# Splitting the second score products of two attention maps over the two halves of TensorE's rows

## The chip, the cores and the metric

The kernel runs on one core of a Trainium2 chip. The metric is the device time in microseconds (us) of one execution, from the median of several runs. The core has five engines that run side by side, each in the order of its own instructions: TensorE does matrix products (PE in the profile, its weight loads are PEld), VectorE does elementwise work and reductions (DVE), ScalarE does activations and copies (ACT), GpSimd does small elementwise work and indirect transfers (POOL), and SyncE issues most transfers (SP). They wait for each other through semaphores.

## The reference, cut to what matters

The reference is a two-layer transformer on 256 image tokens and 256 context tokens of width 1024. Each layer normalizes and modulates the tokens, projects them, runs three kinds of attention heads in parallel, projects back, and runs a mixture of 16 experts. The change lies in the scores of the attention:

```
def diff_attention(q, k, v, lam):          # "A" heads: two maps each
    s = jnp.einsum('bhiqd,bhikd->bhiqk', qb.astype(jnp.float32), kf) * scale
    p = jax.nn.softmax(s, axis=-1)
    w = p[:, :, 0] - lam * p[:, :, 1]
...
def gqa_attention(q, k, v, sink=None):     # "B" heads: two query heads share a key head
    s = jnp.einsum('bhgqd,bhkd->bhgqk', qb.astype(jnp.float32), kf) * scale
...
def window_attention(q, k, v, kc, vc, sink):   # "C" heads: a band mask, and a sink
```

All of it is in float32, with heads of 64 dimensions. Layer 0 computes attention for the context tokens too; layer 1 only for the image tokens.

## The kernel before, in words

The tokens lie in four tiles of 128: tiles 0 and 1 are the context, tiles 2 and 3 the image. A context tile attends to 256 keys (`nk` = 2 blocks), an image tile to 512 (`nk` = 4). Attention is cut into items: one `AItem` per query tile and A head (two maps), one `BItem` per query tile and pair of B or C heads (two maps as well). Layer 0 has 32 items, of which the second 16 are of image tiles; layer 1 has 16, all of image tiles. So 32 items have 512 keys.

Products of float32 are made from parts. A number is split into a high part, rounded to the kernel's float32r, and a low part, the rest. For the keys, `to_T` (L874) writes for map `i` the high part of the 64 dimensions into one half of the 128 partitions (the half `64*i`) and the low part into the other half. For the queries, both halves of the partitions hold the same 64 dimensions; `Item.high` (L1446) makes their high part and `Item.low` (L1453) their low part, both on GpSimd. One product over 128 rows with the high part of the queries thus gives high times high plus high times low; a second one with the low part of the queries gives low times high plus low times low. `Item.maps` (L1457) does this: for each of the two maps it makes the two products one after the other into the map's PSUM bank (L1466), and for masked C items it then adds the mask with a small bf16 product over 128 columns (L1470). The context items put both maps into one bank; the image items take two banks.

The scores' banks come from a ring of three (`PS_ATT`, L47, `sc=3`), and an image item takes two, so that one of its two maps has to wait until the exponentials of an earlier map have left its bank.

After the scores, `maxima` (L1472) reduces each map over its keys on VectorE (L1480, one instruction per map for 512 keys), then scales the maxima (L1486, or L1483 and L1484 with a sink). `exps` (L1488) runs the exponentials on ScalarE (L1493). `weights` combines the maps (L1534 for A items) or normalizes them (L1619, L1620), `transposes` turns them on TensorE (`tp`, L193), `evacuate` copies them out, and `values` multiplies them with the values (`poA`, L1549, in tiles of 128x128 of the array; `poB`, L1640, in tiles of 128 rows by 64 columns).

The order is written out by hand in `attention` (L954) with `TICK` (L65). In each tick TensorE gets, in this order: the transposes of item n, the transposes of an earlier tile's end (`onA`) where there are any, the scores of item n + 3, the values of item n - 1, and then some units of other work, the modulation products `ada` (L459, 128 rows by 32 columns of the array), as many as `fill` deals out. So right after an image item's scores TensorE meets `poA` or a transpose (the whole array), or `poB` or `ada` (the array cut by columns). VectorE gets in each tick the sums and weights of item n first, and then the maxima of item n + 3.

One product elsewhere has the form that the change brings: near the end of layer 1, `add` (L1274) adds the ninth group of experts with `sT[s]` and `y[s]` (L1282), where `s` is the lower or the upper 64 rows in turn, each into a bank of its own.

Of the kernel before, what the change touches and what calls it, by code (L numbers as in the profile page):

```python
# [1429 lines left out]
class Idle:  # L1430

    high = low = weights = scores = transposes = maxima = evacuate = exps = sums = values = staticmethod(lambda: None)
# [3 lines left out]
class Item:  # L1436
# [20 lines left out]
    def maps(self, kT, k, mask=None):  # L1457
        m, nc = self.m, self.nc
        if self.nk == 2:
            self.banks = [m.bank("sc").rearrange("p (i n) -> p i n", i=2)]  # L1460
            self.ps = [self.banks[0][:, i] for i in range(2)]
        else:
            self.ps = [m.bank("sc"), m.bank("sc")]
        for i, ps in enumerate(self.ps):
            for n, part in enumerate(self.hl):
                nc.tensor.matmul(ps, lhsT=part[:, i], rhs=kT[:, k, i, :self.nkey],  # L1466
                                 start=n == 0, stop=n == 1 and mask is None)
            if mask is not None:
                c, v = mask
                nc.tensor.matmul(ps[:, c * 128:c * 128 + 128], lhsT=m.k["identb"], rhs=v, start=False, stop=True)  # L1470

    def maxima(self):  # L1472
# [538 lines left out]
```

## Time and profile before

| | |
|---|---|
| median of 3 runs | 889.74 us (887.74 to 889.86) |
| the profiled execution | 888.22 us |
| its span, from the first to the last instruction | 886.3 us |
| TensorE busy | 784.3 us, 88% of the span |
| VectorE busy | 582.4 us, 66% |
| ScalarE busy | 447.6 us, 50% |
| GpSimd busy | 222.2 us, 25% |
| granted TensorE clock, mean | 0.95 of full speed |

Busy time says how long an engine had something in it; since products overlap in the array, a busy TensorE is not one at its peak. What sets the time is read from the chain of work that ended last, which goes back from the last instruction to whatever released it, step by step. Start times are counted from the beginning of the span. A timeline row of several instructions gives the first start and the time to the last end, so that the distance between the starts of two rows, not their lengths, tells how long the first kept the engine from the second.

### The profile page before, as it was taken

The numbers are of one execution on the slowest core, as the hardware profiler recorded it, in microseconds if no ns is written. First come the engines' busy times: TensorE is split into PE (matmuls) and PEld (weight loads), VectorE is DVE, ScalarE is ACT, GpSimd is POOL, SyncE is SP. The second block draws the span as 40 slices with busy tenths as digits, with TensorE's granted clock in tenths as the row PEclk, the third lists the DMA queues.
The fourth block names the chain that finished last, engine by engine and source line by source line (L and its number), as shares of the span: only waits on it lengthen the run. The fifth ranks groups of instructions, "written<-read, shape, count | busy, mean of one in ns | idle before, by whom it ended". The sixth has DMA issues, their size and how long they took to land.

```text
span 886.3 us, 12972 instructions
## 1 busy us (share of the span) xinstructions
PE 784.3 (88%) x4731; PEld 576.3 (65%) x4731; DVE 582.4 (66%) x1200; ACT 447.6 (50%) x861; POOL 222.2 (25%) x258
## 2 busy tenths in 40 slices
PE   4899999889989977999999549998899797999984
PEld 0578878445557746999999438887555565656541
DVE  1577673879863798899999586697667566221226
ACT  2454442667773416888888546462466543111112
POOL 2000101556320133443342472100423101000200
PEclk9999999999999988999999859999899997999987
DMA  9952221667879337899993757342188955999981
GB/s 319 344 185 96 95 96 48 247 270 284 275 214 376 121 148 263 306 388 401 400 408 156 249 195 292 128 158 95 51 331 215 340 186 215 350 423 422 419 333 51
DMA packets 54505, 219.18 MB, mean 247 GB/s; under 512 B 10299, under 2 KB 10299, under 8 KB 36640
## 3 DMA queue, kind: packets, MB, share of 16 engines
q1 hardware_dynamic: 40816, 182.34, 55.0%
q0 software_dynamic: 8736, 24.92, 7.9%
q10 hardware_dynamic: 4880, 11.00, 3.2%
q8 instruction: 39, 0.64, 0.3%
q14 instruction: 34, 0.28, 0.1%
HBM read 207.09 MB, written 16.84 MB: 253 GB/s over the span
## 4 chain that ended last, share of the span: by engine, by line
PE 66%; DVE 16%; DMA 8%; ACT 3%; issue 3%; POOL 2%; SPq 0%; ACTq 0%; POOLq 0%; DVEq 0%
PE mm L207 7%; PE mm L206 7%; PE mm L205 7%; PE tp L193 6%; PE gu L1189 6%; PE ada L459 4%; PE gu L207 4%; PE gu L205 3%; PE gu L206 3%; DMA wraw<-in_w_up 3%; PE sc L1466 3%; PE w L1245 3%; DVE wlo L235 2%; PE w L1154 2%; DVE nm L1480 2%
## 5 line engine op out<-in xcount | busy, mean ns | idle before, releaser
L235 DVE TENSOR_TENSOR wlo<-wraw,whi 128x1024 fp32r<-128x1024 f32 x136 | 186.1, 1392 | 43.0 <-ACT whi L234 40.5
L234 ACT CAST whi<-wraw 128x1024 fp32r<-128x1024 f32 x152 | 152.8, 1050 | 57.7 <-PE mm L207 35.5
L205 PE MATMUL mm<-whi,Xh 128*128 128x512 f32 x288 | 116.3, 405 | 5.1 <-ACT Xh L690 4.7
L206 PE MATMUL mm<-wlo,Xh 128*128 128x512 f32 x288 | 115.3, 400 | 0.5 <-DVE wlo L235 0.5
L207 PE MATMUL mm<-whi,Xl 128*128 128x512 f32 x288 | 115.0, 399 | 0.5 <-DVE Xl L694 0.5
L221 POOL TENSOR_TENSOR rstd<-ms,cst 128x1 f32<-128x1 f32 (+2 forms) x34 | 29.4, 864 | 272.1 <-DVE ms L219 263.2
L1493 ACT ACTIVATE e<-sc,nm 128x512 f32<-128x512 f32 (+1 forms) x96 | 58.4, 613 | 42.4 <-DVE nm L1486 22.6
L207 PE MATMUL gu<-whi,xl 128*128 128x256 f32 x256 | 74.3, 290 | 0.0
L205 PE MATMUL gu<-whi,xh 128*128 128x256 f32 x256 | 74.2, 290 | 0.0
L206 PE MATMUL gu<-wlo,xh 128*128 128x256 f32 x256 | 72.7, 284 | 0.0
L1189 PE MATMUL gu<-wraw,xq 128*64 128x256 f32 x512 | 64.4, 396 | 3.7 <-DMA wraw<-in_w_up 3.7
L205 PEld LDWEIGHTS mm<-whi,Xh 128*128 128x128 f32 x288 | 55.1, 191 | 18.7 <-ACT Xh L690 6.2
L207 PEld LDWEIGHTS mm<-whi,Xl 128*128 128x128 f32 x288 | 55.0, 191 | 13.9 <-DVE Xl L694 1.5
L206 PEld LDWEIGHTS mm<-wlo,Xh 128*128 128x128 f32 x288 | 55.1, 191 | 12.8 <-DVE wlo L235 1.2
L235 POOL TENSOR_TENSOR wlo<-wraw,whi 128x1024 fp32r<-128x1024 f32 x16 | 42.7, 2672 | 81.1 <-ACT whi L234 50.3
L1189 PEld LDWEIGHTS gu<-wraw,xq 128*64 128x64 f32 x512 | 37.9, 142 | 24.1 <-DMA wraw<-in_w_up 4.2
L193 PEld LDWEIGHTS tp<-ident,e 128*128 128x128 f32 x240 | 26.1, 142 | 40.8 <-issue 21.1
L1480 DVE TENSOR_REDUCE nm<-sc 128x1 f32<-128x512 f32 x64 | 41.2, 684 | 16.5 <-PE sc L1466 11.6
L207 PEld LDWEIGHTS gu<-whi,xl 128*128 128x128 f32 x256 | 49.3, 193 | 1.1 <-DVE xl L1050 0.4
L205 PEld LDWEIGHTS gu<-whi,xh 128*128 128x128 f32 x256 | 49.6, 194 | 0.3 <-ACT xh L1049 0.3
L206 PEld LDWEIGHTS gu<-wlo,xh 128*128 128x128 f32 x256 | 49.5, 193 | 0.0
L193 PE MATMUL tp<-ident,e 128*128 128x128 f32 x240 | 37.8, 286 | 8.4 <-DVE e L1534 3.9
(348 smaller groups left out, 1625.4 us busy)
## 6 DMA issues: line engine op xcount, KB each, us to landing
wraw<-in_w_ada SPq DMA_DIRECT2D x40, 1024.0 KB, 4.9
wraw<-in_w_gate SPq DMA_DIRECT2D x32, 1024.0 KB, 10.1
wraw<-in_w_up SPq DMA_DIRECT2D x32, 1024.0 KB, 11.0
wraw<-in_w_down SPq DMA_DIRECT2D x32, 1024.0 KB, 14.1
wraw<-in_w_in SPq DMA_DIRECT2D x14, 1024.0 KB, 5.2
wraw<-in_w_ada SPq DMA_DIRECT2D x16, 512.0 KB, 8.1
yrows<-y ACTq DMA_DIRECT2D x16, 512.0 KB, 8.1
wraw<-in_w_in POOLq DMA_DIRECT2D x5, 1024.0 KB, 11.9
```

The lines of the kernel that those rows point to most:

```text
L193: self.nc.tensor.transpose(out, in_, self.k["ident"][:n, :n])
L205: mm(out, lhsT=xh, rhs=wh, start=start, stop=False)
L206: mm(out, lhsT=xh, rhs=wl, start=False, stop=False)
L207: mm(out, lhsT=xl, rhs=wh, start=False, stop=stop)
L221: nc.gpsimd.tensor_tensor(r, ms, self.k["mhalf"][:, :width], OP.pow)
L234: nc.scalar.copy(h, raw[:, lo:hi])
L235: (engine or nc.vector).tensor_tensor(l, raw[:, lo:hi], h.bitcast(F32), OP.subtract)
L459: nc.tensor.matmul(ps[32 * j:32 * j + 32, :], lhsT=self.silu_c[:, kc, :], rhs=raw[:, 512 * j:512 * j + 512], start=kc == 0, stop=kc == NKC ...
L1189: nc.tensor.matmul(gu[PSLOTS * g:PSLOTS * g + PSLOTS, 256 * b:256 * b + 256], lhsT=xq[q][:, kc, c:c + PSLOTS], rhs=raw[:, kc * 256:kc * 25 ...
L1245: nc.tensor.matmul(y[hf][gs], lhsT=hT[:, c, 0:PSLOTS] if p == NP else hT[:, c, gs], rhs=raw[:, c * D + o * 512:c * D + o * 512 + 512], sta ...
L1480: V.reduce_max(self.nm[:, i:i + 1], self.ps[i], axis=AX.X)
L1493: nc.scalar.activation(self.e[i][:, :self.nkey], self.ps[i], AF.Exp, scale=0.125, bias=self.nm[:, i:i + 1], accum_out=self.z[i])
```

## The change

For items with 512 keys the two first products, each over 128 rows, come first, one for each map; then the two second products come, each over 64 rows: map 0 on rows 0 to 63 and map 1 on rows 64 to 127, where the high part of its keys lies. The low times low part is no longer computed there. The masks follow after both. Items with 256 keys keep their products and their order. The numbers of products, weight loads and columns stay the same.

```diff
-        for i, ps in enumerate(self.ps):
-            for n, part in enumerate(self.hl):
-                nc.tensor.matmul(ps, lhsT=part[:, i], rhs=kT[:, k, i, :self.nkey],
-                                 start=n == 0, stop=n == 1 and mask is None)
-            if mask is not None:
-                c, v = mask
+        high, low = self.hl
+
+        def product(i, part, rows, **flags):
+            nc.tensor.matmul(self.ps[i], lhsT=part[rows, i], rhs=kT[rows, k, i, :self.nkey], **flags)
+
+        if self.nk == 2:
+
+            for i in range(2):
+                product(i, high, slice(0, 128), start=True, stop=False)
+                product(i, low, slice(0, 128), start=False, stop=True)
+            return
+        for i in range(2):
+            product(i, high, slice(0, 128), start=True, stop=False)
+
+        for i in range(2):
+            product(i, low, slice(64 * i, 64 * i + 64), start=False, stop=mask is None)
+        if mask is not None:
+            c, v = mask
+            for ps in self.ps:
                 nc.tensor.matmul(ps[:, c * 128:c * 128 + 128], lhsT=m.k["identb"], rhs=v, start=False, stop=True)
```

## Rows read from the trace of the kernel before

**Rows 1.** The page's chain that ended last: shares of the span by engine.

```profile
PE 66%; DVE 16%; DMA 8%; ACT 3%; issue 3%; POOL 2%; SPq 0%; ACTq 0%; POOLq 0%; DVEq 0%
```

**Rows 2.** Busy time by stretch, image items: window, length, engines, granted clock, DMA.

```profile
197.00:264.00 67.00, 61.35 (x433) 37.67 (x433) 52.99 (x137) 49.78 (x122) 25.31 (x42) 1.00 0.76 263
626.00:689.00 63.00, 57.93 (x387) 33.63 (x385) 46.25 (x109) 39.77 (x100) 24.43 (x42) 0.95 0.67 217
...
626.00:638.00 12.00, 8.92 (x30) 4.07 (x29) 10.47 (x21) 5.06 (x14) 9.36 (x17) 0.72 0.01 1
```

**Rows 3.** The instructions of line L1466: count, shortest, median and longest ns.

```profile
L1466 PE MATMUL sc<-kT,qhl x96: 277/395/792, 154.6 to 666.4; 128*128 128x512 f32 x64, 128*128 128x256 f32 x32
...
L1466 PE MATMUL sc<-k2T,qhl x96: 277/396/792, 155.6 to 684.9; 128*128 128x512 f32 x64, 128*128 128x256 f32 x32
```

**Rows 4.** Timeline of PE around two unmasked items: start, length, line, array tile, count.

```profile
215.25 1.17 PE L1466 MATMUL sc<-kT,qhl 128*128 128x512 f32 x4
216.26 1.05 PE L1549 MATMUL poA<-vA,ptA 128*128 128x128 f32 x8
...
218.65 1.16 PE L1466 MATMUL sc<-k2T,qhl 128*128 128x512 f32 x4
219.75 1.06 PE L459 MATMUL ada<-wraw,silu_c 128*32 128x512 f32 x8
```

**Rows 5.** Timeline of PE around L1282, whole-array products and then products of 64 rows.

```profile
870.96 1.08 PE L1282 MATMUL acc<-yl,sT 128*128 128x512 f32 x4
...
871.97 0.50 PE L1282 MATMUL acc<-yh,sT 64*128 64x512 f32 x2
...
872.30 0.40 PE L1282 MATMUL acc<-yh,sT 64*128 64x512 f32 x2
```

**Rows 6.** The chain by time, dense products before layer 1's attention: start, us, what.

```profile
624.01 0.23 PE mm L205
```

**Rows 7.** Timeline of PE around a masked item.

```profile
670.34 0.71 PE L1466 MATMUL sc<-k2T,qhl 128*128 128x512 f32 x2
670.89 0.23 PE L1470 MATMUL sc<-mask,identb 128*128 128x128 bf16 x1
670.93 0.71 PE L1466 MATMUL sc<-k2T,qhl 128*128 128x512 f32 x2
671.49 0.23 PE L1470 MATMUL sc<-mask,identb 128*128 128x128 bf16 x1
671.55 0.33 PE L1549 MATMUL poA<-vA,ptA 128*128 128x128 f32 x1
```

**Rows 8.** Timeline of PE and DVE at layer 0's first image item.

```profile
197.02 1.18 PE L1466 MATMUL sc<-kT,qhl 128*128 128x512 f32 x4
...
197.77 1.29 DVE L1480 TENSOR_REDUCE nm<-sc 128x1 f32<-128x512 f32 x2 [1.39 <-PE sc L1466]
```

**Rows 9.** The chain by time, layer 0, image items.

```profile
197.77 1.30 DVE nm L1480 x2
...
204.72 1.21 DVE nm L1480 x2
...
207.03 0.73 PE sc L1466 x2
...
215.49 0.93 PE sc L1466 x4
...
218.89 0.92 PE sc L1466 x4
...
249.66 1.30 DVE nm L1480 x2
```

**Rows 10.** The chain by time, layer 1, its first image items.

```profile
629.45 0.75 PE sc L1466 x2
...
630.22 0.70 DVE nm L1480
...
632.73 1.24 DVE nm L1480 x2
...
635.21 1.22 PE sc L1466 x2
```

**Rows 11.** Timeline of PE in the same stretch, third item.

```profile
632.01 1.22 PE L1466 MATMUL sc<-k2T,qhl 128*128 128x512 f32 x2 [1.04 <-ACT e L1493]
```

**Rows 12.** Waits, layer 1's image items: who for whom, us, times, longest.

```profile
DVE nm L1480 <- PE sc L1466: 6.0, 5, 2.0
```

## The prediction

> **What bounds the kernel now.** I read the chain that ended last first: 66% of it is TensorE and 16% VectorE [rows 1]. So a product that gets cheaper can count, but only in the stretches where the change is. These are the image items of the two layers, 67 and 63 us long, with TensorE busy 61.35 and 57.93 us and VectorE 52.99 and 46.25 us [rows 2]: TensorE is nearly full, VectorE is close behind, and the chain passes between them. The line of the scores has 64 + 64 products of 512 columns [rows 3], four for each of 32 items. Half of them, 64, become products of 64 rows, that is 32 pairs; the others stay.
>
> What one item keeps TensorE from doing next is the distance between starts in the timeline. With four score products followed by `poA`, which uses the whole array, it is 216.26 - 215.25 = 1.01 us; followed by `ada`, which cuts the array by columns, 219.75 - 218.65 = 1.10 us [rows 4]. A whole-array product in a dense run takes 0.23 us [rows 6], so the first of the four takes 1.01 - 3 x 0.23 = 0.32 us, and a passage to another cut of the array costs 1.10 - 1.01 = 0.09 us. That 0.09 is the number to watch, because the new pair is another cut.
>
> **The change part by part.** The pair itself. The kernel already has such pairs, at L1282: four whole-array products from 870.96, then two products of 64 rows that both start at 871.97, then two more at 872.30 [rows 5]. Two things are to be seen. The two halves run side by side, since two take 0.50 us from start to end and the next two start 0.33 us later. And the passage costs the same 0.09: 871.97 - 870.96 - 4 x 0.23. The 0.33 instead of 0.23 is a weight load that nothing hides just after the passage. So the pair saves one product (0.23) and pays 0.09 to go in, 0.10 for the bare weight load, and 0.09 to come out, unless the next product cuts the array anyway. No row shows the way out of a pair; I take the 0.09 of the other passages, with 0 and 0.18 as ends. Beside that, the first whole-array product after the pair shows its own weight load: between 0 and the 0.10 of the pair, I take 0.05.
>
> The sum for an item on TensorE is then 0.32 (first product of map 0) + 0.23 + 0.09 (first product of map 1, passage) + 0.33 + 0.09 (pair, passage) = 1.06 us. Before `ada` or `poB` that replaces 1.10: a gain of 0.04. Before `poA` or a transpose it is 1.06 + 0.05 = 1.11 and replaces 1.01: a loss of 0.10. A masked item takes 671.55 - 670.34 = 1.21 us now [rows 7]; after, 1.06 and two masks in a row, of which the second ends 0.06 before `poA` starts as now, and the first takes 0.05 to 0.12 by the same rows: 1.17 to 1.24, which I count as 0.
>
> On the price of a passage the Trainium skill has a rule ("TensorEngine Tiling (Array Packing)", Key Properties): changing the tiling mode, not just the tile, drains TensorE. The 0.09 of rows 4 and 5 agrees that there is a price. The Trainium skill's page "TensorE: Matmul & The Clock Gate" (Step-by-step) puts the drain at about 128 cycles, an estimated 0.05 us at 2.4 GHz; with that the sum below would come out about 1 us lower. The rows measure it here, so I stay with 0.09.
>
> The order. Before, map 0 was complete after two products, and VectorE could reduce it while TensorE made map 1; now both maps are complete together, after the pair. In the first image item the reduction starts 197.77 - 197.02 = 0.75 us after the scores [rows 8]. After, it is 0.32 + 0.23 + 0.09 + 0.50 (the first pair's length) + the 0.03 that a reduction starts after the end of the product, = 1.17: 0.42 us later. Map 1 is not earlier by anything that counts, since VectorE reduces the maps one after the other (1.30 for two [rows 9]).
>
> The bank. The three banks make one of the maps wait for exponentials. Before, that wait stood ahead of the third product; now it stands ahead of the second, and the pair is queued behind it, so map 0's second product waits with it, and VectorE's reduction of map 0 behind that.
>
> Now along the chain, where it passes through scores. (a) Through all four products to TensorE's next work: six unmasked items to the whole array (215.49 is one), 6 x 0.10 = +0.60; four to a column cut (218.89 is one), 4 x -0.04 = -0.16; five masked ones, 0. (b) From a bank that comes free through the products to TensorE's next work: 207.03 and one such in layer 1. Before, 0.34 + 0.23 = 0.57; after, 0.34 + 0.09 + 0.33 + 0.09 = 0.85: 2 x 0.28 = +0.56. (c) Through the scores to the reductions, where VectorE stood idle: 197.77 and one like it, 2 x 0.42 = +0.84; 249.66, where the mask too now comes behind the pair, +0.50; at 204.72 and one more item VectorE was only just later than the scores, 0 to 0.42 each, I take 0.20, +0.40. (d) The start of layer 1 [rows 10, 11]. There TensorE, VectorE and ScalarE have little else, and each item waits for a bank of the one before. First item: the first product has its weights ready there, +0.27. Second: its high product gets the bank at 629.45; before, only map 1's reduction was left (done at 630.92); after, the pair ends 0.34 + 0.09 + 0.50 = 0.93 later, then both reductions follow, 1.30: at 631.72, +0.80. Third: bank at 632.01, but VectorE began the reductions only at 632.73, since it was busy; after, the pair at the slow clock of this stretch (0.72 granted on average [rows 2], between the levels 1.2 and 2.4 GHz; the two products take 1.22 in all [rows 11]) ends some 1.4 us after the bank, +0.65. Fourth (635.21): +0.15. Together +1.87.
>
> Sum: -0.16 + 0.60 + 0.56 + 1.74 + 1.87 = +4.6 us. What is off the chain hides in the other engine's work, and no edit adds work to VectorE, ScalarE, GpSimd or a transfer. The attention's end feeds the output projection directly in both layers, so I count the delays in full. The sum is made on the profiled execution: 888.2 + 4.6 = 892.8; that one lies 1.5 below the median of the runs, so the forecast is 889.7 + 4.6 = 894.3 us.
>
> **The rivals.** First, not slower: the late reductions are absorbed. VectorE waits for scores 6.0 us in five places in layer 1 [rows 12], and if the work behind these waits has slack, terms (c) and (d) vanish and (a) and (b) stay, +1.0: 890.7. It decides as soon as each reduction has 0.4 us to spare. Against it stands that the chain itself passes through these reductions, so there is none there.
>
> Second, the passage is free and the weight load hidden, since the products before and after use the same columns. Then each of the 15 items of (a) saves 0.23, -3.45; (b) is 0.34 + 0.23, 0; the reductions are late by 0.20 instead of 0.42, +0.6 in (c) and some +0.9 in (d): -1.9, so 887.8. Against it: rows 5 show 0.09 and 0.33 for just this form. The Trainium skill's rule that points here ("TensorE: Matmul & The Clock Gate", Measured speedup vs the span model) has packed tiles cost one product's time and some 4 ns for each further tile; the pair's own 0.50 agrees, but that model has no passage in it.
>
> Third, the change doesn't do what it says: the halves run one after the other, because they read other operands than L1282's. Then each pair costs 0.23 more, at the 26 places of (a) to (d) (15, 2, 5 and 4), +6.0: 900.3. Rows 5 speak against it.
>
> **How the numbers follow.** What a measurement of this kernel can tell from no change is about 0.3%, 2.7 us. The forecast has 0.66 (slower 0.62, within 0.3% 0.04), the absorbed delay 0.18 (0.17 within), the free passage 0.10 (half within, half faster), the halves in turn 0.06. That gives slower 0.68, within 0.3% 0.26, faster 0.06. The low end takes in the absorbed delay (890.7), less 1.0 if the passages were free in the way out and the bare load of `poA` 0, less 0.7 for the runs' own spread: 889.0. The high end takes the forecast with 0.18 for the way out at the 13 places where the whole array follows (six, five and two; 13 x 0.09 = +1.2), a start of layer 1 that stays at the slow clock for one more item's products (+1.2), and half the spread of the runs shown (1.1): 898.
>
> **What would show it.** The scores' second products as 64x512 pairs with equal starts; about 1.1 us from the first score product to `poA` and 1.06 to `ada`; the first reduction 1.17 after the first product; longer waits of VectorE for scores. If the pair starts 0.23 after the product before it and `poA` 0.23 after the pair, the passage is free and I am wrong. If the stretches show these delays but end no later, they were absorbed.

## The result, and the profile after

The median went from 888.74 us (885.39 to 889.86, four runs) to 897.35 us (896.06 to 899.39, four runs): a ratio of 1.0105, with a 95% interval of 1.007 to 1.014. The kernel is 8.6 us slower where +4.6 had been forecast. The profiled execution took 897.12 us, its span is 895.2 us, and the mean granted clock is 0.947.

The page's chain that ended last has TensorE at 66% and VectorE at 16%, the shares of [rows 1], so it tells nothing of where the time went. Busy time by stretch does. Here each layer's image items are one stretch, from the first score product to the first product of the output projection (window, length, then PE, PEld, DVE, ACT, POOL busy with their counts, granted clock, DMA share, GB/s). First the kernel before:

```profile
197.00:266.40 69.40, 62.36 (x439) 38.08 (x437) 54.05 (x138) 51.13 (x125) 25.53 (x42) 1.00 0.77 263
625.90:700.60 74.70, 65.37 (x443) 38.40 (x441) 52.66 (x128) 46.74 (x113) 28.44 (x49) 0.95 0.72 232
```

and then the kernel after:

```profile
195.20:269.40 74.20, 65.41 (x440) 36.84 (x438) 53.63 (x139) 51.15 (x125) 25.51 (x42) 0.98 0.74 250
630.60:709.90 79.30, 67.11 (x444) 36.49 (x442) 51.19 (x128) 46.57 (x113) 27.70 (x49) 0.94 0.65 221
```

By the starts themselves the stretches grew by 4.74 and 4.61 us, 9.35 together; the rest of the span is 0.5 shorter. So the whole loss lies in the two stretches, half in each. VectorE and ScalarE have no more to do in them than before, VectorE even 0.4 and 1.5 us less.

The pair itself came out as forecast. In the forms of the score products' line, the 64 products of 64 rows stand where half of the 128-row ones of [rows 3] stood (count, shortest, median and longest ns, first and last start, forms):

```profile
L1467 PE MATMUL sc<-kT,qhl x96: 277/477/792, 155.2 to 675.0; 128*128 128x256 f32 x32, 128*128 128x512 f32 x32, 64*128 64x512 f32 x32
L1467 PE MATMUL sc<-k2T,qhl x96: 278/477/794, 156.1 to 693.9; 128*128 128x256 f32 x32, 128*128 128x512 f32 x32, 64*128 64x512 f32 x32
```

Next TensorE's timeline around the same two unmasked items as in [rows 4]. A row of four score products prints the tile of the first; two of them are 64 by 128:

```profile
214.07 1.14 PE L1467 MATMUL sc<-kT,qhl 128*128 128x512 f32 x4
215.14 1.16 PE L1562 MATMUL poA<-vA,ptA 128*128 128x128 f32 x8
...
217.63 1.14 PE L1467 MATMUL sc<-k2T,qhl 128*128 128x512 f32 x4
218.70 1.06 PE L459 MATMUL ada<-wraw,silu_c 128*32 128x512 f32 x8
```

From start to start that is 1.07 us ahead of the whole array (1.01 before, 1.11 forecast) and 1.07 ahead of a column cut (1.10 before, 1.06 forecast). Inside the first item the starts follow each other after 313, 327, 3 and 430 ns: the second first-product needs 0.33 with the way in, the pair starts together, and 0.43 later the next work begins. A masked item, as in [rows 7]:

```profile
240.30 1.14 PE L1467 MATMUL sc<-k2T,qhl 128*128 128x512 f32 x4
...
241.50 0.33 PE L1562 MATMUL poA<-vA,ptA 128*128 128x128 f32 x1
```

1.20 us where it took 1.21. And the first image item of layer 0, as in [rows 8]:

```profile
195.22 1.13 PE L1467 MATMUL sc<-kT,qhl 128*128 128x512 f32 x4
195.84 0.19 PEld L1467 LDWEIGHTS sc<-kT,qhl 64*128 64x128 f32 x2 [0.35 <-issue]
196.38 1.29 DVE L1493 TENSOR_REDUCE nm<-sc 128x1 f32<-128x512 f32 x2 [1.39 <-PE sc L1467]
```

The reduction starts 1.16 us after the scores, 0.75 before and 1.17 forecast. The middle row shows the pair's bare weight loads: the loader sat idle for 0.35 us ahead of them, and for nothing that the profile names.

So the prices of a single item are right or nearly so (ahead of the whole array 0.06 measured against 0.10), and the sum is still only half of the loss. What grew is waiting. Waits of TensorE's weight loads for ScalarE's exponentials (that is, for a bank of the scores) and of VectorE for scores, kernel before (us, times, longest), in layer 0's stretch and then in layer 1's:

```profile
PEld sc L1466 <- ACT e L1493: 2.1, 5, 0.8
DVE nm L1480 <- PE sc L1466: 5.7, 5, 2.0
...
PEld sc L1466 <- ACT e L1493: 6.5, 5, 1.9
```

Layer 1's row for VectorE is [rows 12], 6.0. The same after:

```profile
PEld sc L1467 <- ACT e L1506: 4.2, 6, 0.9
DVE nm L1493 <- PE sc L1467: 7.9, 7, 2.2
...
PEld sc L1467 <- ACT e L1506: 9.7, 7, 2.8
DVE nm L1493 <- PE sc L1467: 12.5, 9, 2.4
```

TensorE waits 2.1 and 3.2 us longer for banks, VectorE 2.2 and 6.5 us longer for scores. One place shows how, the seventh and eighth image items of layer 0. The kernel before:

```profile
219.39 1.29 DVE L1480 TENSOR_REDUCE nm<-sc 128x1 f32<-128x512 f32 x2 [0.73 <-PE sc L1466]
220.92 0.69 ACT L1493 ACTIVATE e<-sc,nm 128x512 f32<-128x512 f32 x1 [0.32 <-DVE nm L1486]
221.50 0.19 ACT L1493 ACTIVATION_READ_ACCUMULATOR e<-sc,nm 128x1 f32 x1
221.59 1.18 PE L1466 MATMUL sc<-kT,qhl 128*128 128x512 f32 x4
222.34 1.29 DVE L1480 TENSOR_REDUCE nm<-sc 128x1 f32<-128x512 f32 x2
```

The seventh item's scores start at 218.65 [rows 4]. Its reductions follow 0.74 later, its first exponential is done at 221.69, and the bank that this frees is wanted by the third product of the eighth item, at 222.14: 0.45 us to spare. After:

```profile
218.80 1.29 DVE L1493 TENSOR_REDUCE nm<-sc 128x1 f32<-128x512 f32 x2 [1.33 <-PE sc L1467]
220.12 0.27 DVE L1499 TENSOR_SCALAR nm<-nm 128x2 f32<-128x2 f32 x1
220.42 0.69 ACT L1506 ACTIVATE e<-sc,nm 128x512 f32<-128x512 f32 x1 [1.01 <-DVE nm L1499]
220.54 0.48 PE L1467 MATMUL sc<-kT,qhl 128*128 128x512 f32 x1
221.01 0.19 ACT L1506 ACTIVATION_READ_ACCUMULATOR e<-sc,nm 128x1 f32 x1
221.25 0.94 PE L1467 MATMUL sc<-kT,qhl 128*128 128x512 f32 x3 [0.22 <-ACT e L1506]
222.22 1.29 DVE L1493 TENSOR_REDUCE nm<-sc 128x1 f32<-128x512 f32 x2 [0.73 <-PE sc L1467]
```

The reductions follow 1.17 after the scores (217.63), the exponential is done at 221.20, and the bank is now wanted by the second product, at 220.54 + 0.32 = 220.86. It starts at 221.25, 0.39 late, with the pair behind it, and the next reductions wait for that pair. The 0.45 to spare became 0.34 too little, and the product starts 0.05 after the bank is free. The reductions come 0.43 later, the bank is wanted 0.23 sooner in its item, the eighth item itself starts 0.03 sooner after the seventh, and the stretch from the reductions to the bank is 0.10 longer, since VectorE's scaling of the maxima (L1499, L1486 before) took 0.27 us instead of 0.17.

This scaling is a link of the loop too, and not a steady one. In the kernel before, 15 of the 32 scalings of items with 512 keys took over 0.2 us, up to 1.1, the others 0.16 to 0.20; 14 of the 15 ended 22 to 31 ns after a GpSimd instruction that ran beside them (most often L1455, the low part of later queries). In the kernel after it is 7 of 32, all ending 17 to 30 ns after one. That GpSimd holds the scaling up is read from these ends; no run tested it by itself.

### The profile page after: what moved, and what is told of

It reads as the page before. It is cut to its first block, busy times and chain, and to the rows that moved or that the text cites. A ratio compares the mean times of both kernels' runs of the same rounds, so it can differ in the third digit from the quotient of the medians.

```text
span 895.2 us, 12974 instructions
## 1 busy us (share of the span) xinstructions
PE 788.8 (88%) x4731; PEld 573.0 (64%) x4731; DVE 580.8 (65%) x1200; ACT 446.9 (50%) x861; POOL 221.2 (25%) x258
## 4 chain that ended last, share of the span: by engine, by line
PE 66%; DVE 16%; DMA 6%; ACT 4%; issue 4%; POOL 3%; ACTq 0%; SPq 0%; POOLq 0%; DVEq 0%
PE mm L206 7%; PE mm L207 7%; PE mm L205 7%; PE tp L193 6%; PE gu L1189 6%; PE gu L207 4%; PE sc L1467 4%; PE ada L459 3%; PE gu L205 3%; PE gu L206 3%; PE w L1245 3%; DVE nm L1493 2%; DMA wraw<-in_w_up 2%; DVE wlo L235 2%; PE poB L1653 2%
```

## The experiments

The theory after these readings ("O") was that the order of the four products costs most of the loss, through this loop of scores, reductions, exponentials and banks; the rival ("P") that TensorE's own time does, through the pair's passages and weight loads. All kernels below were timed beside the kernel before on the same chip. The stretches are again those from the first score product of the image items to the output projection, in the profiled execution.

| kernel | ratio to before | 95% interval | layer 0, us | layer 1, us |
|---|---|---|---|---|
| before | 1 | | 69.4 | 74.7 |
| after | 1.0105 | 1.007 to 1.014 | 74.1 | 79.3 |
| order_only | 1.007 | 1.0052 to 1.0088 | 71.8 | 77.5 |
| map1_first | 1.0054 | 1.0034 to 1.0074 | 71.9 | 77.7 |
| one_half | 1.0082 | 1.005 to 1.0113 | 72.5 | 80.2 |
| first_only | 0.9957 | 0.9939 to 0.9976 | 67.7 | 74.1 |
| early_scale | 0.9966 | 0.9943 to 0.9989 | 68.8 | 71.5 |
| early_after | 1.0056 | 1.0039 to 1.0074 | 71.1 | 77.9 |
| order_early | 1.0014 | 0.9994 to 1.0035 | 71.5 | 74.7 |
| early_all | 0.9957 | 0.9938 to 0.9975 | 68.8 | 71.5 |
| four_before | 1.0326 | 1.0293 to 1.0359 | 84.3 | 81.0 |
| four_after | 1.0498 | 1.0452 to 1.0544 | 90.6 | 88.6 |

**order_only.** The new order with second products over 128 rows: no pair, no passage.

```diff
-            product(i, low, slice(64 * i, 64 * i + 64), start=False, stop=mask is None)
+            product(i, low, slice(0, 128), start=False, stop=mask is None)
```

> The order of the changed kernel, but both second products over all 128 rows: no passages to another cut of the array, no pair side by side. Theory O (the loss of the change, 8.6 us by the medians, comes from the order: map 0 is complete late and its second product stands behind the wait for map 1's bank): map 0's reduction is late by some 0.24 us instead of 0.42 where no bank is waited for, and by about as much as in the change where one is, so 4 to 7 us over the kernel before remain, with waits of over 0.3 us ahead of map 1's first product in about as many items as after the change. Theory P (the loss comes from the passages and the bare weight loads of the pair): TensorE does the same work as in the kernel before, so no change within 1.5 us.

894.84 us against 887.61, 0.70% slower by the ratio: the order alone costs about two thirds of what the change costs (5.2 of the 9.35 us by the stretches of the table). P as the main cause has fallen. At the eighth image item there is a wait for the bank again, without any pair. First GpSimd and VectorE's scaling of the seventh item, then TensorE:

```profile
220.83 0.73 POOL L1455 TENSOR_TENSOR qhl<-qT,qhl 128x256 fp32r<-128x256 f32 x1
220.98 0.61 DVE L1499 TENSOR_SCALAR nm<-nm 128x2 f32<-128x2 f32 x1
221.63 0.48 PE L1467 MATMUL sc<-kT,qhl 128*128 128x512 f32 x1
222.45 0.97 PE L1467 MATMUL sc<-kT,qhl 128*128 128x512 f32 x3 [0.35 <-ACT e L1506]
```

The second product starts 0.82 us after the first, 0.50 of it a wait. The order's own part would hardly have done this here: map 0's reduction is 0.25 later (1.00 after the scores, 0.74 before) and the bank is wanted 0.23 sooner, together just over the 0.45 to spare. The other 0.44 is the scaling, 0.61 us instead of 0.17, which ends 24 ns after GpSimd's instruction. At items 2 and 12 the scaling ahead took its 0.17, and the kernel before had nothing to spare (it waited 0.04 us there); so the waits of 0.50 at these two items are the order's own. Where the starts of the items fall behind those of the kernel before, counted from the layer's first image item (us):

| start of | after | order_only | map1_first | one_half | first_only | early_scale |
|---|---|---|---|---|---|---|
| layer 0, item 3 | 0.60 | 0.46 | 0.46 | 0.24 | -0.37 | -0.14 |
| item 8 | 0.76 | 0.25 | 0.45 | 0.65 | -0.69 | -0.41 |
| item 9 | 1.42 | 0.86 | 0.85 | 1.03 | -1.15 | -0.41 |
| item 12 | 1.53 | 0.87 | 0.87 | 1.80 | -2.49 | -0.41 |
| item 13 | 2.40 | 1.32 | 1.34 | 2.07 | -2.46 | -0.54 |
| item 16 | 2.68 | 1.41 | 1.69 | 2.89 | -3.19 | -0.23 |
| output projection | 4.74 | 2.40 | 2.51 | 3.09 | -1.73 | -0.60 |
| layer 1, item 4 | 1.75 | 1.69 | 1.26 | 0.65 | -0.21 | -1.60 |
| item 5 | 2.92 | 2.63 | 0.62 | 1.75 | 0.21 | -2.94 |
| item 9 | 3.87 | 2.82 | 1.41 | 3.72 | -0.84 | -2.62 |
| item 12 | 3.83 | 2.82 | 1.41 | 3.91 | -1.32 | -2.62 |
| item 13 | 4.23 | 3.05 | 2.98 | 4.30 | 1.23 | -3.24 |
| item 16 | 4.63 | 2.86 | 3.03 | 5.16 | -0.16 | -3.21 |
| output projection | 4.61 | 2.78 | 3.03 | 5.43 | -0.63 | -3.22 |

The kernel after and order_only lose time in jumps, at the same items: 2, 8 and 12 of layer 0. These are items whose second product waits for its bank (0.73, 0.39 and 0.73 us in the kernel after) and which waited at most 0.05 us for one before.

**map1_first.** The kernel before, with its reductions in the other order. TensorE's products stay as they were, and so does the product that waits for the bank; only VectorE begins with the map that is complete last.

```diff
-            for i in range(2):
+            for i in (1, 0):
                 V.reduce_max(self.nm[:, i:i + 1], self.ps[i], axis=AX.X)
```

> The kernel before, but VectorE reduces map 1 first and then map 0, for items with 512 keys. TensorE's instructions and their order are those of before; both reductions now wait for the whole of the scores, as after the change, while the wait for the bank stands where it stood. Theory O, if the late reductions are what makes the exponentials and with them the banks late: 4 to 8 us over the kernel before. If instead the place of the wait on TensorE is what counts (map 0's second product behind it): under 2 us. Theory P: no change within 1.5 us.

892.23 us, 0.54% slower, nearly as much as the order, with jumps at the same items 2, 8 and 12 of layer 0 (columns two and three of the table). So late reductions alone can cost this much. They are 0.46 us late here, though, about as in the kernel after (0.42) and twice as late as in order_only (0.23 to 0.25), where the bank is also wanted 0.23 sooner; at items 2 and 12 both kernels wait 0.50 us. How the price of the order divides between late reductions and the place of the bank's wait is therefore not shown. At the eighth item the wait now stands ahead of the third product of the old order:

```profile
222.39 1.58 PE L1466 MATMUL sc<-kT,qhl 128*128 128x512 f32 x4
223.81 0.38 PE L1549 MATMUL poA<-vA,ptA 128*128 128x128 f32 x2
```

1.42 us from the scores to `poA`, where an unhindered item takes 1.01 [rows 4]; 0.23 of this is again a longer scaling (0.40 us, ending 24 ns after L1455).

**one_half.** The old order, with only map 1's second product on 64 rows: passages in and out and the bare load, but no second half beside it and map 0 complete as early as before.

```diff
-                nc.tensor.matmul(ps, lhsT=part[:, i], rhs=kT[:, k, i, :self.nkey],
+                rows = slice(64, 128) if self.nk == 4 and i == n == 1 else slice(0, 128)
+                nc.tensor.matmul(ps, lhsT=part[rows, i], rhs=kT[rows, k, i, :self.nkey],
```

> The kernel before with its order, but map 1's second product (the last of the four) over 64 rows: it pays the way into another cut of the array, the bare weight load and the way out, as the pair does, and saves no product. Leaves out low times low of map 1 only. Theory P: at least the loss of the change, 8.6 us, and 0.23 us more per item on the chain, so 11 to 15 us. Theory O: only TensorE's time at the places where it bounds, 0.28 us for six items before the whole array, 0.19 for four before a column cut, about 0.2 for five masked ones, and some for two waits: 3 to 5 us.

895.65 us, 0.82% or 7.3 us slower, between the two expectations. An item in front of `poA`:

```profile
222.01 1.36 PE L1467 MATMUL sc<-kT,qhl 128*128 128x512 f32 x4
223.30 1.16 PE L1550 MATMUL poA<-vA,ptA 128*128 128x128 f32 x8
```

1.29 us instead of 1.01, so 0.28 for one passage in, the bare load and one passage out. The table shows another shape than that of the order: it creeps, by 0.15 to 0.4 at most items from the eighth on in layer 0, and has its largest steps at the start of layer 1. TensorE's time thus counts at more items than the 15 of term (a). The changed kernel pays the same passages but saves a product for them, which leaves 0.06 ahead of the whole array and -0.03 ahead of a column cut.

**first_only.** The kernel before without the second products of the items with 512 keys: low parts of the queries are left out there, and TensorE has 64 products less.

```diff
-            for n, part in enumerate(self.hl):
+            for n, part in enumerate(self.hl[:1] if self.nk == 4 else self.hl):
...
-                                 start=n == 0, stop=n == 1 and mask is None)
+                                 start=n == 0, stop=(n == 1 or self.nk == 4) and mask is None)
```

> The kernel before without any second product for items with 512 keys: the low part of the queries is left out of these scores. 0.46 us of TensorE less per item, and both maps complete earlier. Both theories: 6 to 11 us under the kernel before. It tells what the two second products cost in all, and so that a pair that is free could have saved about half of that at most.

885.0 us, only 0.43% or 3.8 us faster by the ratio, less than was expected of either theory. Layer 0's items gain up to 3.19 us by the sixteenth; layer 1's gain 1.32 by the twelfth and lose 2.55 in that one item. Busy time in the stretch around it (columns as above) and TensorE's timeline, first in the kernel before, which comes to this item some 5 us later:

```profile
662.00:673.00 11.00, 9.13 (x62) 5.64 (x66) 9.93 (x27) 7.42 (x19) 5.16 (x9) 1.00 0.42 153
...
666.08 0.74 PE L1466 MATMUL sc<-kT,qhl 128*128 128x512 f32 x2 [1.02 <-ACT e L1493]
...
667.63 1.92 PE L459 MATMUL ada<-wraw,silu_c 128*32 128x512 f32 x16
```

And without the second products:

```profile
657.00:668.00 11.00, 8.50 (x40) 4.58 (x41) 8.30 (x22) 6.56 (x18) 5.01 (x8) 0.69 0.35 124
...
661.23 0.80 PE L1466 MATMUL sc<-kT,qhl 128*128 128x512 f32 x1 [1.26 <-ACT e L1493]
...
663.66 3.60 PE L459 MATMUL ada<-wraw,silu_c 128*32 128x512 f32 x16
```

The granted clock is 0.69 instead of 1.00: for part of the stretch TensorE ran at 1.2 GHz, after a wait of 1.26 us for a bank. Sixteen `ada` products take 3.60 us instead of 1.92. The kernel before waits 1.02 us for the same bank and keeps its clock. That the longer wait and the thinner work led to the lower clock is read from this order in time and was not tested by itself.

**four_before, four_after.** A fourth bank for the scores, taken from the transposes, in both kernels.

```diff
-PS_ATT = dict(sc=3, ada=1, tp=2, poA=1, poB=1)
+PS_ATT = dict(sc=4, ada=1, tp=1, poA=1, poB=1)
```

> The kernel before with four banks for scores in the attention instead of three; the bank is taken from the transposes, which keep one of two. A control for the next run: its own time can go either way, between 3 us under and 15 us over the kernel before, since transposes then wait for each other's copies.

> The changed kernel with four banks for scores and one for transposes. To be compared with the run before it. Theory O (the wait for map 1's bank, in front of map 0's second product, carries the loss): with four banks each item's two maps have banks of their own for one item ahead, that wait goes, and the difference to the control is 0 to 4 us, not 8.6. Theory P: the passages are all there, so the difference stays 7 to 10 us.

918.51 and 932.45 us, against 888.06: 13.9 us apart, more than before and not less. As a test it decides nothing, because taking the bank away from the transposes put another wait in the place of the one removed. One row of the waits of four_before between 195 and 280 us, most of layer 0's image items (1.9 us, 2 times, in the kernel before):

```profile
PEld tp L193 <- ACT ptB L1630: 17.1, 12, 2.1
```

TensorE's transposes now wait 17.1 us for ScalarE to empty their only bank, and ScalarE is where late reductions arrive. The changed kernel also ran at a lower clock here (0.92 and 0.88 in the two stretches, against 0.98 and 1.00). What the order costs with enough banks for everything was not tried.

**early_scale.** If late reductions cost through the loop, a shorter loop should gain, with TensorE's work untouched. In the kernel before, the first exponential waits until both maps are reduced and scaled. Here each map without a sink is scaled right after its own reduction, one small instruction more per item:

```diff
+        if self.nk == 4 and self.sink is None:
+            for i in range(2):
+                nm = self.nm[:, i:i + 1]
+                V.reduce_max(nm, self.ps[i], axis=AX.X)
+                V.tensor_scalar(nm, nm, -0.125, None, OP.mult)
+            return
```

> The kernel before, but for items of 512 keys without a sink each map's maximum is scaled right behind its reduction, so that the exponentials of map 0 can start some 0.6 us before map 1 is reduced. If the loop from bank to scores, reduction, exponentials and back to the bank bounds stretches of the attention, 1 to 4 us under the kernel before; if it does not, 0 to 2 us over it, for 24 more small instructions of about 0.17 us on VectorE.

884.09 us against 888.06, 0.34% or 3.0 us faster than the kernel before by the ratio. The seventh and eighth image items of layer 0 again:

```profile
217.95 1.17 PE L1466 MATMUL sc<-k2T,qhl 128*128 128x512 f32 x4
218.69 0.69 DVE L1479 TENSOR_REDUCE nm<-sc 128x1 f32<-128x512 f32 x1 [0.85 <-PE sc L1466]
...
219.61 0.69 ACT L1499 ACTIVATE e<-sc,nm 128x512 f32<-128x512 f32 x1
...
220.89 1.18 PE L1466 MATMUL sc<-kT,qhl 128*128 128x512 f32 x4
```

The exponential starts 1.66 us after the scores instead of 2.27, and its 0.69 end at 220.30, before the next item begins at 220.89. The gain lies almost wholly in layer 1 (-3.2 of -3.8), where the banks were waited for longest. It has two possible sources, and no run separates them: the exponential of map 0 starts a reduction sooner, and none of the scalings of these 32 items took over 0.16 us here, where 15 took 0.2 to 1.1 in the kernel before.

**early_after, order_early.** The same edit in the kernel after and in order_only, to see what of the loss stays when the loop is short.

> The changed kernel with each map's maximum scaled right behind its reduction (items without a sink), as in early_scale. Theory O, in its sharper form: the loss sits in the loop from a bank through scores, reductions and exponentials back to the bank. The early scaling takes one reduction (0.6 us) out of this loop, so 3 to 7 us under the changed kernel (890 to 894). But map 0 still needs the pair, which stands behind the wait for map 1's bank, so the loop still contains TensorE's wait and it stays 5 to 10 us over early_scale. Theory P (passages): the same 8.6 us over early_scale as the change over before, and under 3.5 us less than the changed kernel.

> Order of the changed kernel, all second products over 128 rows, and the early scaling. Its distance to early_scale is the order alone once a reduction is out of the loop, its distance to early_after is the pair with its passages. Theory O: 2 to 6 us over early_scale, from the place of the wait; early_after lies another 2 to 5 us above it, since the pair is complete some 0.2 us later than the whole second products. Theory P: within 1.5 us of early_scale, and early_after 7 us or more above it.

893.49 us (+0.56%) and 890.66 us (+0.14%, an interval of 0.9994 to 1.0035). Over early_scale, from the ratios of the table, that is +0.90% and +0.48%, where the long loop had 1.05% and 0.70%. These differences lie inside the intervals (together some 0.4 points, an estimate from the table), and in the profiled stretches the order costs 5.9 us over early_scale against 5.2 over the kernel before. So it is not shown that a shorter loop takes any part of the loss away. The order still has a price of its own: order_early is not within 1.5 us of early_scale, as P had it. Nor does this price hang on held scalings alone, since in early_scale and order_early none took over 0.16 us. The pair on top of the order costs 0.42% here, which is clear of the intervals, and 0.35% with the long loop (1.0105 against 1.007), which is not; some 3 to 4 us in both.

**early_all.** Early scaling for the items with a sink too.

> The kernel before with the early scaling in all 32 items, those with a sink too. If the loop bounds masked items as well, 0.5 to 2 us under early_scale, so 3 to 6 under the kernel before; if it does not, the same as early_scale within 1 us.

885.14 us, a ratio of 0.9957: the same as early_scale within the intervals, and like it faster than both kernels of the case. The waits of weight loads for banks are down from 2.1 and 6.5 us in the two stretches to 0.2 and 3.6, as they are in early_scale.

## Why the prediction was right in direction and short by half

**The pair: right.** A way in of 0.09 and a bare load of 0.10 gave 1.06 us ahead of a column cut (1.07 measured) and 1.11 ahead of the whole array (1.07, so I took 0.04 too much for the way out and `poA`'s load). With masks nothing changes, as forecast (1.20 against 1.21). The free passage has fallen: the second first-product takes 0.32 to 0.33 us, not 0.23. The halves do not run in turn either: they start 2 to 5 ns apart.

**The order: right as a price where nothing waits.** Map 0 is reduced 1.16 us after the scores (1.17 forecast). The absorbed delay has fallen: late reductions alone cost 0.54% (map1_first). That attention's end feeds the output projection, so that delays count in full, held too: nothing of the 9.35 us came back after the stretches, beyond 0.5 in the rest.

**The step that failed** is this one: "What is off the chain hides in the other engine's work". Apart from the start of layer 1, the prediction priced the delay at five places where the chain passed through a reduction, and the bank at the two where it passed through a wait. But the loop scores, reductions, scaling, exponential, bank, next item's scores had little slack beside the chain: none at items 2 and 12, and 0.45 us at the eighth, of which the change takes 0.43 + 0.23 and a longer scaling 0.10. So the loop became the bound at items where no wait had stood. The terms against what was measured:

- Layer 0, 2.24 forecast, 4.74 measured. Where a bank wait was on the chain the price held: at 207.03, the fourth item [rows 9], +0.28 was forecast for it and its start to the next one's start grew by 0.30. But the jumps at items 2, 8 and 12 (0.65, 0.66 and 0.87) come from waits that were not there, and the end from the sixteenth item's start on took 2.06 more. The sixteenth's second product now waits 0.50 too. In the kernel before, the chain ran beside that item's scores; after, it passes through them and their reductions, as its rows in order of time show:

```profile
253.96 0.43 PE sc L1467 x2
...
254.60 1.30 DVE nm L1493 x2
```

- Term (d), the start of layer 1, 1.87 forecast. The first three items together come out, 0.27 + 0.80 + 0.65 = 1.72 against 1.75, but piece by piece they do not, and the agreement is partly luck. Counted from the layer's first product, the product that waits for its bank starts as early as before in the second item (634.12 less 630.57, before 629.45 less 625.89; +0.27 forecast) and 1.26 later in the third (637.94, before 632.01; +1.07 forecast). The difference is the scaling, which the prediction left as it was: 0.30 shorter in the first item (0.19 us for 0.49) and 0.46 longer in the second (0.66 for 0.20). For the fourth +0.15 was forecast and 1.17 came. Its row after:

```profile
640.15 0.78 PE L1467 MATMUL sc<-kT,qhl 128*128 128x512 f32 x1
641.85 1.52 PE L1467 MATMUL sc<-kT,qhl 128*128 128x512 f32 x3 [0.92 <-ACT e L1506]
```

The second product waits 1.70 us from the first for its bank, and TensorE, which had waited through the three items before as well, is still at 1.2 GHz. The granted clock over ten microseconds, kernel before and then after:

```profile
631.00:641.00 10.00, 8.71 (x42) 4.84 (x42) 8.91 (x20) 6.07 (x16) 5.92 (x11) 0.67 0.20 63
```

```profile
636.00:646.00 10.00, 7.14 (x24) 3.22 (x24) 6.51 (x16) 4.44 (x12) 4.52 (x8) 0.50 0.01 2
```

The range had such an item at the slow clock in its high end (+1.2); here it is in the result.

- The rest of layer 1, 0.50 forecast (2.37 less 1.87), 1.69 measured: again waits at items that had none on the chain.

**What stays open.** The order is the larger part, 0.70% of 1.05%, within the intervals of both. The other 0.35% (3.1 us) goes with the pair. It is not known how it divides between TensorE's own time (passages at more items than I counted, as one_half's creeping shows) and the pair completing about 0.2 us later than two whole second products, which feeds the same loop. Nor did a run separate the slow clock at the start of layer 1 from the waits that go with it, or keep GpSimd's instructions away from the scalings.

## What to carry to other kernels

Before reordering products on a full engine, ask when each result is complete and follow it around to the buffer that it frees: read the time to spare of that loop at several items, and not only on the chain that ended last, for reductions 0.46 us late in every item cost 4.8 us (map1_first), where the chain's five places had been priced at 1.74. Read the small instructions of the loop at several items too: the scaling here took between 0.16 and 1.1 us. Two products on half the rows each save one product's time but pay a way in, a bare weight load and a way out, so a single pair about breaks even (1.07 us, against 1.01 ahead of the whole array and 1.10 ahead of a column cut). Where such a loop is the tight place, let the first consumer start on the first half: scaling each maximum at once gained 0.34% with one more instruction per item, though some of that may be scalings no longer held up.

## What the runs showed of the hardware

The way in costs the same in every item that doesn't wait for its bank, 316 to 329 ns where a dense whole-array product takes 230; after a bank wait, at the full clock, it is 416 to 435, which is the 0.34 + 0.09 that term (b) had assumed. VectorE's scaling of two maxima takes 0.16 to 0.20 us, or ends some 20 to 30 ns after a GpSimd instruction that ran beside it, up to 1.1 us in all (14 of 32 in the kernel before, 7 in the kernel after). Less work on TensorE did not mean a proportionally shorter time: first_only left out 64 products of 0.23 us each, 14.7 in all, and gained 3.8, with the granted clock of its layer 1 stretch at 0.88 instead of 0.95.
